# Softmax sums squared eight at a time, decay operands built four heads at a time, and a convolution tap on ScalarE, in a two-layer hybrid diffusion block on one core

## The chip, the core and the metric

The kernel runs on one core of one Trainium2 chip. The core has five engines that run their own instruction queues in order: TensorE (PE in the rows, its weight loads PEld), VectorE (DVE), ScalarE (ACT), GpSimd (POOL) and SyncE (SP, which here only issues DMAs). The metric is device microseconds of one execution. Everything told below about the kernel before comes from its times, its profile page, its trace and the order of its instructions.

## What is computed

Two layers over 1024 latent tokens and 256 context tokens of width 1024, all in float32. Cut to what matters here:

```python
for l in range(2):
    h = rms_norm(x) * (1 + sc1) + sh1
    q.., x_ssm, dt = split(h @ w_in[l])           # one wide projection
    y_na  = neighbourhood_attention(...)           # 4 heads
    y_df  = rms_norm(softmax(q1 k1) v - lam * softmax(q2 k2) v)   # 4 heads, "differential"
    u     = silu(depthwise_conv(x_ssm, 5 taps))    # the SSM's convolution
    y_ssm = ssd_chunked(u, dt)                     # 10 chunks of 128, 8 heads, both directions
    x = x + g1 * (concat(y_na, y_df, y_ssm) @ w_out[l])
    h = rms_norm(x) * (1 + sc2) + sh2
    gate, val = split(h @ w_up[l])
    x = x + g2 * ((silu(depthwise_conv(gate, 3 taps)) * val) @ w_down[l])
```

In the SSM, a decay matrix exp(cs_i - cs_j) of 128 by 128 is needed for each head, chunk and direction. In the differential attention the kernel never divides the scores by the first softmax sum s0: it lets the norm that follows cancel it, and for that adds 64 * eps * s0^2 to the mean square.

## The kernel before

The big projections are split into high and low parts, so that each product is three matmuls (lines 390 to 392 for the input, up and out projections, 1232 to 1234 for the down projection). For each weight block SyncE loads it, ScalarE rounds the high part (`wH`, line 240) and GpSimd subtracts to get the low part (`wL`, line 241).

The stages of a layer follow each other: the SSM's projections with their convolution (`xbc_conv`, lines 519 to 532, eight blocks of 128 channels); chunk states and the z projection; the projections of differential and neighbourhood attention, with the SSM's output (`ssd_out`, line 905) interleaved as a background stream (I call this the SSD stage); then the two attentions side by side (`df_stream`, line 678, and `natt`, line 1032); the output projection; the feed-forward part (`ffn`, line 1168), where for each of 22 blocks the gate is projected, convolved (line 1194 to 1198), passed through SiLU and multiplied into the value projection.

The order on each engine is not written by hand: a scheduler places instructions by priority and by its own estimate of times, and each engine then runs its own list in order, waiting at semaphores.

- Convolutions. ScalarE copies the projection from PSUM into a padded tile (`pad`, line 515; `fpad`, line 1184). VectorE computes the first tap with the bias (line 524, line 1194), then adds the other taps (line 527 four times, line 1197 twice) in place in `cacc` or `fa`. ScalarE applies SiLU.
- Decay. `decay(g)` (line 950) builds for two directions d and two halves e of a split number an operand `mf` of 128 by 4 heads by 128: a triangular mask times one column of `lah` for each head. Per tile that is four instructions of 128 columns, two on VectorE and two on GpSimd (line 958). A matmul (line 960) consumes each tile; there are three `mf` buffers. ScalarE then takes the exponential and VectorE multiplies it into `M` (line 965), which line 980 consumes. Over both layers there are 18 chunks, so 36 decays, 144 tiles and 576 instructions.
- Differential attention. A unit is one query tile of one head; there are 40 units in layer 0 and 32 in layer 1. For each, TensorE makes the scores of the two softmaxes (line 719, two PSUM buffers `s`), VectorE moves them out of PSUM with a running maximum (line 720), ScalarE takes exp and leaves the sums in `sums` (two columns), VectorE forms `rho` (lines 727 and 728) and the column 64 * eps * s0^2 in `dg` (line 733), GpSimd combines the two maps (line 736 scales, line 738 adds), TensorE transposes and multiplies with the values. After four query tiles, line 783 adds `dg` into the mean square.

Of the kernel before, what the change touches and what calls it, by code (L numbers as in the profile page):

```python
# [10 lines left out]
F32 = mybir.dt.float32  # L11
# [69 lines left out]
def hybrid_kernel(ctx, tc, xin, cc, w_ada, bada, gmf, w_in, w_dt, w_out, w_up, w_dn, vec, cst, rope, nab, out):  # L81
# [171 lines left out]

# [1 line left out]

# [72 lines left out]

# [1 line left out]
    def norm_temps(pool):  # L330
# [52 lines left out]

# [1 line left out]
    def proj_chunk(wh, wl, c0, n, evac, order=range(KT)):  # L385
# [45 lines left out]
    def dfproj(l, dfv, qchunks, lam, gq, gnq, sub, lam_init):  # L431
        NT = 10
        with phase(f"dp_{l}", "right") as p:
            rp = p.tile([128, 2, SEQ], F32, name="rp")
            SP.dma_start(out=rp, in_=rope)
            # lambda and gains
            lv = vc[:, l, V_LAM:V_LAM + 128].rearrange("p (a d) -> p a d", a=4)
# [45 lines left out]
    def mixer(l):  # L483
# [16 lines left out]

# [1 line left out]
        with phase(f"m1_{l}") as p:  # L502
            pads = []
            for i in range(2):
                pd = p.tile([128, 1288], F32, name=f"pad{i}")
                for a, b in ((0, 2), (1026, 1030), (1286, 1288)):
                    G.memset(pd[:, a:b], 0.0)
                pads.append(pd)

            def xbc_ev(b):  # L510
                pd = pads[b % 2]

                def ev(ps, c0, n):
                    o = 2 + c0 if c0 < SEQ else 1030
                    S.copy(out=pd[:, o:o + n], in_=ps)

                return ev

            def xbc_conv(b):
                pd = pads[b % 2]  # L520
                a = p.tile([128, 1284], F32, tag="cacc", name="cacc", bufs=2)
                cw = V_CW + 5 * b
                W = 1284 if full or b < 6 else SEQ
                V.tensor_scalar(out=a[:, 0:W], in0=pd[:, 0:W], scalar1=vcol(l, cw), scalar2=vcol(l, V_CB + b),
                                op0=ALU.mult, op1=ALU.add)
                for j in range(1, 5):
                    V.scalar_tensor_tensor(out=a[:, 0:W], in0=pd[:, j:j + W], scalar=vcol(l, cw + j), in1=a[:, 0:W],
                                           op0=ALU.mult, op1=ALU.add)
                act(out=a[:, 0:W], in_=a[:, 0:W], func=ACTF.Silu)
                SP.dma_start(out=ud[l][b, :, 0:SEQ], in_=a[:, 0:SEQ])  # L530
                if W > SEQ:
                    SP.dma_start(out=ud[l][b, :, SEQ:T], in_=a[:, 1028:1284])

            ws = w_pre if l == 0 else [load_w(w_in[l, B_XBC + b]) for b in range(2)]
            proj_many(ws, ALLC, [xbc_ev(b) for b in range(2)])
            for b in range(2):
                xbc_conv(b)
            if l == 0:
                side[0] = ada_stream(0, range(2, 5), asx.enter_context(phase("as", "right")))
            side_step(1)  # L540
            for b in range(2, 8):
                proj(w_in[l, B_XBC + b], ALLC if full or b < 6 else MAINC, xbc_ev(b))
                xbc_conv(b)
                side_step(1)

# [1 line left out]
        exp_tables()  # L547
        da = ExitStack()
        dfv = da.enter_context(phase(f"dfv{l}")).tile([128, NT, 256], F32, name="dfv")
        with phase(f"sw{l}") as sp:  # L550
# [58 lines left out]
          if True:  # L609
            p = sp  # L610
            ssd_states(l, p, dte, tot, full)

# [1 line left out]
            silu_tables()  # L614

            def zblk(b):
                def ev(ps, c0, n):
                    z = p.tile([128, 512], F32, tag="z", name="z", bufs=2)
                    act(out=z[:, :n], in_=ps, func=ACTF.Silu)
                    SP.dma_start(out=zd[l][b, :, c0:c0 + n], in_=z[:, :n])  # L620

                proj(w_in[l, B_Z + b], qchunks, ev)

            for b in range(4):
                zblk(b)
                side_step(2)
            side_finish()
            asx.close()
            exp_tables()
# [5 lines left out]

# [1 line left out]
        npx = ExitStack()  # L637
# [36 lines left out]
        nv_p = nvx.enter_context(phase(f"nv_{l}", "right"))  # L674
# [1 line left out]
        p = da.enter_context(phase(f"da_{l}"))  # L676

        def df_stream():
# [4 lines left out]
            po = {}  # L683
            dgs = {}

# [19 lines left out]
            def scores(b, qt, hh):  # L705
# [5 lines left out]
                es = []  # L711
                sums = p.tile([128, 2], F32, tag="sums", name="sums", bufs=4)
                for m in range(2):
# [3 lines left out]
                    for ci, (c, n) in enumerate(kch):  # L717
# [10 lines left out]
                V.scalar_tensor_tensor(out=rho, in0=rho, scalar=sums[:, 0:1], in1=lam,  # L728
                                       op0=ALU.mult, op1=ALU.mult)
                if hh == 0 and qt % 4 == 0:  # L730
                    dgs[b, qt // 4] = p.tile([128, 8], F32, tag="dg", name="dg", bufs=2)
                u = qt % 4 * 2 + hh
                V.scalar_tensor_tensor(out=dgs[b, qt // 4][:, u:u + 1], in0=sums[:, 0:1], scalar=64 * EPS, in1=sums[:, 0:1],
                                       op0=ALU.mult, op1=ALU.mult)
# [22 lines left out]
            def values(b, qt):  # L757
# [19 lines left out]
                sq, oh = tl("dsq"), tl("doh", F32R)  # L777
                act(out=sq, in_=pv, func=ACTF.Square)
                pm = pst("t", 2)[:, :n]
                PE.matmul(pm, C(C_BD64), sq, start=True, stop=False)  # L780
                for i in range(gn):
                    for hh in range(2):
                        PE.matmul(pm[64 * hh:64 * hh + 64, i * 128:(i + 1) * 128],
                                  dgs[b, qt // 4][:, 2 * i + hh:2 * i + hh + 1].to_broadcast([128, 64]), ident,
                                  start=False, stop=(i == gn - 1))
# [30 lines left out]

# [1 line left out]
        open_mm(ns=2, nt=1)  # L818
# [86 lines left out]
    def ssd_out(l, p, c, dts, lah, ecs):  # L905
# [44 lines left out]
        def decay(g):  # L950
            pd = pst("s", 2)
            i = 0
            for d, mk in ((0, C_PI), (1, C_SI)):
                for e in range(2):
                    mf = p.tile([128, 4, 128], F32R, tag="mf", name="mf", bufs=3)
                    for hh in range(4):
                        h = 8 * d + 4 * g + hh
                        (V if hh % 2 else G).tensor_scalar(out=mf[:, hh], in0=C(mk), scalar1=lah[:, e, c, h:h + 1], scalar2=1.0,
                                        op0=ALU.mult, op1=ALU.mult)
                    PE.matmul(pd, tri[:, d], mf.rearrange("p h i -> p (h i)"), start=(i == 0), stop=(i == 3))  # L960
# [205 lines left out]

# [1 line left out]
    def ffn(l, xt):  # L1168
# [3 lines left out]
        with phase(f"ffn{l}") as p:  # L1172
# [15 lines left out]
            def up(f, gate_done=False):  # L1188
                pad = pads[f % 2]
                if not gate_done:  # L1190
                    proj(w_up[l, 2 * f], chunks, gate_ev(f))
                a = p.tile([128, 1282], F32, tag="fa", name="fa", bufs=1)
                fw = V_FW + 3 * f
                V.tensor_scalar(out=a[:, :W], in0=pad[:, 0:W], scalar1=vcol(l, fw), scalar2=vcol(l, V_FB + f),  # L1194
                                op0=ALU.mult, op1=ALU.add)
                for j in range(1, 3):
# [89 lines left out]

# [1 line left out]
    with phase("n0") as p:  # L1288
# [165 lines left out]
```

## Time and profile before

| | |
|---|---|
| median of 3 runs | 3622.63 us (3618.60 to 3626.59) |
| profiled execution, first to last instruction (the only time that its profile gives) | 3627.4 us |
| TensorE busy | 3433.8 us, 95% |
| VectorE busy | 1950.4 us, 54% |
| GpSimd busy | 1446.3 us, 40% |
| ScalarE busy | 1242.3 us, 34% |
| mean granted TensorE clock | 0.975 |

Busy time is the union of an engine's instructions. "Granted clock" is the TensorE clock as a share of full speed (2.4 GHz; the lower level is 1.2 GHz). A wait row "PE x <- DVE y" sums the time in which TensorE stood idle just before x and what ended it was the end of y.

### The profile page before, as it was taken

To read this page: it belongs to the slowest core of one execution; us is meant where nothing else is said; L and a number is where in the kernel's file an instruction comes from. 1 tells how busy PE (TensorE), PEld (TensorE's weight loads), DVE (VectorE), ACT (ScalarE), POOL (GpSimd) and SP (SyncE) were. 2 spreads that over 40 slices of the span, in tenths; PEclk is the share of its full clock that TensorE was granted. 3 is DMA by queue.
4 is the path that set the end of the run, shared out by engine and by line. 5 is a ranking of instruction groups with operands and counts; after the bars stand their busy time and mean duration, and the time that the engine had idled before them with its cause. 6 is when DMAs were issued, how large, how long until landed. Compare 5 with 4: busy or idle time off the path is not lost. (4 is left out here: it accounts for less than half of the span.)

```text
span 3627.4 us, 49090 instructions
## 1 busy us (share of the span) xinstructions
PE 3433.8 (95%) x18762; PEld 2724.3 (75%) x18762; DVE 1950.4 (54%) x3816; ACT 1242.3 (34%) x2159; POOL 1446.3 (40%) x1092
## 2 busy tenths in 40 slices
PE   7998898899899999999999898998999999999999
PEld 3876676666678888888887676776666777887887
DVE  6735875787373343333335744885784633334333
ACT  4232433777341111111113333344675421221211
POOL 2136563666362222222222326673565532322332
PEclk8999999999999999999999999998999999999999
DMA  8255444753721111111112236447656211111111
GB/s 294 98 199 164 131 126 132 191 152 105 244 83 46 35 41 35 37 39 36 35 35 82 69 114 211 128 128 192 167 156 215 77 53 41 53 47 41 53 47 70
DMA packets 260202, 381.03 MB, mean 105 GB/s; under 512 B 20736, under 2 KB 161152, under 8 KB 259712
## 3 DMA queue, kind: packets, MB, share of 16 engines
q1 hardware_dynamic: 259968, 377.90, 33.8%
q8 instruction: 148, 2.42, 0.3%
q14 instruction: 86, 0.70, 0.1%
HBM read 294.72 MB, written 83.10 MB: 104 GB/s over the span
## 5 line engine op out<-in xcount | busy, mean ns | idle before, releaser
L390 PE MATMUL mm<-hH,wH 128*128 128x512 f32 (+1 forms) x2960 | 1117.6, 379 | 34.2 <-ACT wH L240 7.6
L391 PE MATMUL mm<-hL,wH 128*128 128x512 f32 (+1 forms) x2960 | 1113.2, 376 | 9.5 <-POOL hL L370 5.3
L392 PE MATMUL mm<-hH,wL 128*128 128x512 f32 (+1 forms) x2960 | 1111.4, 376 | 6.2 <-POOL wL L241 6.2
L241 POOL TENSOR_TENSOR wL<-wr,wH 128x1024 fp32r<-128x1024 f32 x220 | 533.2, 2429 | 1218.4 <-ACT wH L240 1195.3
L390 PEld LDWEIGHTS mm<-hH,wH 128*128 128x128 f32 x2960 | 564.7, 191 | 157.6 <-issue 15.1
L391 PEld LDWEIGHTS mm<-hL,wH 128*128 128x128 f32 x2960 | 564.4, 191 | 127.4 <-POOL hL L370 7.8
L392 PEld LDWEIGHTS mm<-hH,wL 128*128 128x128 f32 x2960 | 564.4, 191 | 114.8 <-POOL wL L241 7.7
L240 ACT CAST wH<-wr 128x1024 fp32r<-128x1024 f32 x220 | 228.3, 1048 | 808.1 <-PE mm L1233 471.9
L1237 DVE SCALAR_TENSOR_TENSOR xt<-mm,mods,xt 128x512 f32<-128x512 f32 (+1 forms) x440 | 300.9, 697 | 253.6 <-PE mm L1234 253.1
L1194 DVE TENSOR_SCALAR fa<-fpad,vc 128x1282 f32<-128x1282 f32 (+1 forms) x44 | 111.1, 2526 | 558.6 <-ACT fpad L1184 550.9
L1234 PE MATMUL mm<-gh,wL 128*128 128x512 f32 (+1 forms) x880 | 328.9, 374 | 0.0
L1232 PE MATMUL mm<-gh,wH 128*128 128x512 f32 (+1 forms) x880 | 325.0, 375 | 3.7 <-DVE xt L1237 3.6
L1233 PE MATMUL mm<-gl,wH 128*128 128x512 f32 (+1 forms) x880 | 326.9, 372 | 0.0
L720 DVE TENSOR_SCALAR_CACHE_REDUCE e<-s 128x512 f32<-128x512 f32 (+1 forms) x400 | 228.4, 588 | 88.2 <-PE s L719 85.6
L1208 POOL TENSOR_TENSOR gl<-fa,gh 128x512 fp32r<-128x512 f32 (+1 forms) x110 | 127.6, 1160 | 300.7 <-ACT gh L1207 300.7
L93 ACT ACTIVATE e<-e,nm 128x1280 f32<-128x1280 f32 (+1 forms) x144 | 182.9, 1271 | 53.6 <-DVE nm L723 48.5
L719 PE MATMUL s<-ks,qst 128*128 128x512 f32 (+1 forms) x400 | 161.5, 441 | 39.0 <-DVE e L720 23.4
L1232 PEld LDWEIGHTS mm<-gh,wH 128*128 128x128 f32 x880 | 164.5, 188 | 41.1 <-DVE xt L1237 8.7
L738 POOL TENSOR_TENSOR e<-e 128x1280 f32<-128x1280 f32 (+1 forms) x72 | 193.1, 2684 | 3.4
L1233 PEld LDWEIGHTS mm<-gl,wH 128*128 128x128 f32 x880 | 165.3, 188 | 32.7 <-issue 0.2
L1234 PEld LDWEIGHTS mm<-gh,wL 128*128 128x128 f32 x880 | 165.5, 188 | 32.1
L1206 DVE TENSOR_TENSOR fa<-fa,mm 128x512 f32<-128x512 f32 (+1 forms) x110 | 69.8, 635 | 209.3 <-PE mm L392 151.7
(269 smaller groups left out, 4930.1 us busy)
## 6 DMA issues: line engine op xcount, KB each, us to landing
wr<-in_w_up_dram SPq DMA_DIRECT2D x88, 512.0 KB
wa<-in_w_ada_dram SPq DMA_DIRECT2D x56, 512.0 KB
wr<-in_w_in_dram SPq DMA_DIRECT2D x48, 512.0 KB
wr<-in_w_dn_dram SPq DMA_DIRECT2D x44, 512.0 KB
wr<-in_w_ada_dram SPq DMA_DIRECT2D x40, 512.0 KB
wr<-in_w_out_dram SPq DMA_DIRECT2D x40, 512.0 KB
nbt<-in_nab_dram SPq DMA_DIRECT2D x64, 192.0 KB
ks<-qkd SPq DMA_DIRECT2D x16, 640.0 KB
```

The lines of the kernel that those rows point to most:

```text
L93: ins = S.activation(**kw)
L240: S.copy(out=wh, in_=wr)
L241: (eng or G).tensor_tensor(out=wl, in0=wr, in1=wh.bitcast(F32), op=ALU.subtract)
L390: PE.matmul(ps[:, :n], wh[:, ks], r, start=(i == 0), stop=False)
L391: PE.matmul(ps[:, :n], wh[:, ks], hsl(hL, k, c0, n), start=False, stop=False)
L392: PE.matmul(ps[:, :n], wl[:, ks], r, start=False, stop=(i == KT - 1))
L720: V.tensor_scalar(out=e[:, c:c + n], in0=s_, scalar1=1.0, scalar2=None, op0=ALU.mult, op1=ALU.max, accum_out=mx[:, ci:ci + 1])
L738: G.tensor_tensor(out=es[0][:, 0:nk], in0=es[0][:, 0:nk], in1=es[1][:, 0:nk], op=ALU.add)
L1232: PE.matmul(ps, wh[:, os_], gh[:, c0:c0 + n], start=(i == 0), stop=False)
L1233: PE.matmul(ps, wh[:, os_], gl[:, c0:c0 + n], start=False, stop=False)
L1234: PE.matmul(ps, wl[:, os_], gh[:, c0:c0 + n], start=False, stop=(i == len(hid) - 1))
L1237: V.scalar_tensor_tensor(out=xv, in0=ps, scalar=mods[l][:, 5, o, w:w + 1], in1=xv, op0=ALU.mult, op1=ALU.add)
```

## The change

Three edits. The first convolution tap with its bias becomes an affine activation on ScalarE, in both convolutions: 16 instructions of line 524 and 44 of line 1194 leave VectorE, 60 go to ScalarE. Each `mf` tile is one instruction of 128 by 512 with two broadcast operands, on one engine: of the four tiles of a decay GpSimd makes the first and the last, VectorE the two between. The sums of eight units (four query tiles, two heads) live in one tile, and one instruction squares all eight of them when the group's values are done: 72 instructions of one column become 10 of up to eight.

```diff
-                V.tensor_scalar(out=a[:, 0:W], in0=pd[:, 0:W], scalar1=vcol(l, cw), scalar2=vcol(l, V_CB + b),
-                                op0=ALU.mult, op1=ALU.add)
+                act(out=a[:, 0:W], in_=pd[:, 0:W], func=ACTF.Identity, scale=vcol(l, cw), bias=vcol(l, V_CB + b))
...
-                sums = p.tile([128, 2], F32, tag="sums", name="sums", bufs=4)
+                if hh == 0 and qt % 4 == 0:
+                    sgs[b, qt // 4] = p.tile([128, 8, 2], F32, tag="sums", name="sums", bufs=2)
+                u = qt % 4 * 2 + hh
+                sums = sgs[b, qt // 4][:, u]
...
-                if hh == 0 and qt % 4 == 0:
-                    dgs[b, qt // 4] = p.tile([128, 8], F32, tag="dg", name="dg", bufs=2)
-                u = qt % 4 * 2 + hh
-                V.scalar_tensor_tensor(out=dgs[b, qt // 4][:, u:u + 1], in0=sums[:, 0:1], scalar=64 * EPS, in1=sums[:, 0:1],
-                                       op0=ALU.mult, op1=ALU.mult)
...
                 act(out=sq, in_=pv, func=ACTF.Square)
+                s0 = sgs[b, qt // 4][:, 0:2 * gn, 0]
+                dg = p.tile([128, 8], F32, tag="dg", name="dg", bufs=2)
+                V.scalar_tensor_tensor(out=dg[:, 0:2 * gn], in0=s0, scalar=64 * EPS, in1=s0, op0=ALU.mult, op1=ALU.mult)
...
-                    for hh in range(4):
-                        h = 8 * d + 4 * g + hh
-                        (V if hh % 2 else G).tensor_scalar(out=mf[:, hh], in0=C(mk), scalar1=lah[:, e, c, h:h + 1], scalar2=1.0,
-                                        op0=ALU.mult, op1=ALU.mult)
+                    h = 8 * d + 4 * g
+                    (V if (d + e) % 2 else G).tensor_tensor(
+                        out=mf, in0=C(mk).unsqueeze(1).to_broadcast([128, 4, 128]),
+                        in1=lah[:, e, c, h:h + 4].unsqueeze(2).to_broadcast([128, 4, 128]), op=ALU.mult)
...
-                V.tensor_scalar(out=a[:, :W], in0=pad[:, 0:W], scalar1=vcol(l, fw), scalar2=vcol(l, V_FB + f),
-                                op0=ALU.mult, op1=ALU.add)
+                act(out=a[:, :W], in_=pad[:, 0:W], func=ACTF.Identity, scale=vcol(l, fw), bias=vcol(l, V_FB + f))
```

Since a scheduler sets the order, it moves other instructions too, mostly in the SSD stage and in the attentions. Three places carry the argument. Line numbers of the changed kernel differ by a few.

First, GpSimd in the first chunks of layer 0's SSD stage (`mf` the decay operands, `xd` and `yo` other operands of `ssd_out`, `qn` the rotary product of the attention's projection, `wL` a weight's low part). Before:

```order
L958 TENSOR_SCALAR mf<-cs,lah 128x128 x4
L926 TENSOR_TENSOR xd<-xt,dts 128x512 x2
L958 TENSOR_SCALAR mf<-cs,lah 128x128 x6
L465 TENSOR_TENSOR qn<-qn,rp 128x512
L947 TENSOR_TENSOR yo<-yo 128x512
L958 TENSOR_SCALAR mf<-cs,lah 128x128 x8
```

And with the change:

```order
L926 TENSOR_TENSOR xd<-xt,dts 128x512 x2
L465 TENSOR_TENSOR qn<-qn,rp 128x512
L947 TENSOR_TENSOR yo<-yo 128x512
L957 TENSOR_TENSOR mf<-cs,lah 128x512 x4
L241 TENSOR_TENSOR wL<-wr,wH 128x1024
```

GpSimd's list between two of its other jobs is now a run of two-input instructions of 512 columns and more, where small one-input instructions lay between them.

Second, VectorE in the attentions of layer 0 (`e<-s` moves scores out of PSUM, `nsb` belongs to the neighbourhood attention). Before:

```order
L720 TENSOR_SCALAR e,mx<-s 128x512
L733 SCALAR_TENSOR_TENSOR dg<-sums 128x1
L720 TENSOR_SCALAR e,mx<-s 128x256
L720 TENSOR_SCALAR e,mx<-s 128x512
L723 TENSOR_REDUCE nm<-mx 128x1
```

And with the change, around a stretch that corresponds to it and holds no such instruction:

```order
L730 SCALAR_TENSOR_TENSOR rho<-rho,sums,lam 128x1
L722 TENSOR_SCALAR e,mx<-s 128x256
L722 TENSOR_SCALAR e,mx<-s 128x512
L1097 TENSOR_SCALAR nsb,nmx<-ns 128x256
L725 TENSOR_REDUCE nm<-mx 128x1
```

One `dg` stood in each unit among the moves of the scores; with the change one stands in each group of eight.

Third, ScalarE at the first two blocks of layer 1's SSM convolution. Before:

```order
L240 CAST wH<-wr 128x1024
L515 COPY pad_17137<-mm 128x256
L240 CAST wH<-wr 128x1024
L515 COPY pad_17141<-mm 128x256
L93 ACT_TABLE_LOAD
L93 ACTIVATE cacc<-cacc 128x1284
L515 COPY pad_17137<-mm 128x512 x2
```

And with the change:

```order
L240 CAST wH<-wr 128x1024
L515 COPY pad_16829<-mm 128x256
L93 ACTIVATE cacc<-pad_16829,vc 128x1284
L240 CAST wH<-wr 128x1024
L515 COPY pad_16833<-mm 128x256
L93 ACTIVATE cacc<-pad_16833,vc 128x1284
L93 ACT_TABLE_LOAD
L93 ACTIVATE cacc<-cacc 128x1284
L515 COPY pad_16829<-mm 128x512 x2
```

The two taps stand directly behind the copies that they read; the copies of the third block stand behind the first SiLU as before.

## Rows read from the trace of the kernel before

**Rows 1.** The page: busy us by engine, share of the span, instructions.

```profile
PE 3433.8 (95%) x18762; PEld 2724.3 (75%) x18762; DVE 1950.4 (54%) x3816; ACT 1242.3 (34%) x2159; POOL 1446.3 (40%) x1092
```

**Rows 2.** Windows by stage: length, busy PE, PEld, DVE, ACT, POOL, clock, DMA, GB/s.

```profile
90.00:200.00 110.00, 110.00 (x580) 89.65 (x580) 74.66 (x47) 30.21 (x40) 19.29 (x8) 1.00 0.29 98
300.00:600.00 300.00, 270.21 (x1531) 208.00 (x1531) 229.57 (x470) 113.67 (x230) 183.27 (x233) 0.94 0.42 131
634.00:920.00 286.00, 256.95 (x2194) 189.30 (x2194) 222.69 (x860) 208.67 (x453) 181.39 (x125) 0.98 0.55 151
1075.00:1910.00 835.00, 835.00 (x4280) 704.77 (x4279) 308.96 (x360) 147.54 (x200) 207.01 (x120) 1.00 0.13 38
...
2250.00:2480.00 230.00, 213.80 (x1267) 167.29 (x1268) 182.99 (x368) 89.69 (x177) 147.53 (x188) 0.97 0.46 143
2500.00:2760.00 260.00, 238.25 (x2026) 175.16 (x2025) 205.30 (x783) 191.69 (x374) 167.51 (x99) 0.95 0.58 161
2905.00:3620.00 715.00, 714.86 (x3056) 572.89 (x3055) 261.88 (x281) 135.38 (x170) 204.28 (x106) 1.00 0.16 49
```

**Rows 3.** Waits of TensorE: total us, times, longest us.

```profile
PE s L719 <- DVE e L720: 23.4, 41, 2.1
...
PE s L1002 <- DVE yrs L1001: 8.6, 4, 3.9
...
PE mm L390 <- ACT pad L515: 7.2, 2, 6.2
...
PE o L980 <- DVE M L965: 6.3, 5, 2.3
...
PE s L960 <- DVE mf L958: 5.3, 3, 2.4
...
PE s L960 <- POOL mf L958: 2.0, 5, 0.6
```

**Rows 4.** Groups of instructions by form: busy us, mean ns, idle before.

```profile
L958 POOL TENSOR_SCALAR mf<-cs,lah 128x128 fp32r<-128x128 f32 x288 | 142.6, 512 | 48.3 <-PE s L960 47.5 <-POOL mf L958 0.4
...
L958 DVE TENSOR_SCALAR mf<-cs,lah 128x128 fp32r<-128x128 f32 x288 | 106.5, 429 | 19.7 <-PE s L960 19.4
...
L733 DVE SCALAR_TENSOR_TENSOR dg<-sums 128x1 f32<-128x1 f32 x72 | 67.2, 933 | 12.3 <-ACT e L93 12.2
...
L1194 DVE TENSOR_SCALAR fa<-fpad,vc 128x1282 f32<-128x1282 f32 x22 | 59.3, 2695 | 312.5 <-ACT fpad L1184 308.9 <-POOL gl L1208 3.7
...
L926 POOL TENSOR_TENSOR xd<-xt,dts 128x512 f32<-128x512 f32 x36 | 39.6, 1121 | 48.2 <-PE o L980 43.0 <-DMA xt<-xtd 5.2
...
L965 DVE TENSOR_TENSOR M<-M,cbl 128x512 f32<-128x512 f32 x36 | 31.3, 868 | 0.5
...
L93 ACT ACTIVATE cacc<-cacc 128x1284 f32<-128x1284 f32 x14 | 17.9, 1278 | 77.6 <-DVE cacc L527 67.3 <-issue 10.3
```

**Rows 5.** Timeline, attentions of layer 0: start, us, engine and instruction.

```profile
693.57 2.92 POOL L738 TENSOR_TENSOR e<-e 128x1280 f32<-128x1280 f32 x1
...
694.49 2.02 DVE L733 SCALAR_TENSOR_TENSOR dg<-sums 128x1 f32<-128x1 f32 x1 [1.52 <-ACT e L93]
...
697.17 0.39 PE L719 MATMUL s<-ks,qst 128*128 128x256 f32 x1 [1.98 <-DVE e L720]
```

**Rows 6.** Timeline, SSD stage of layer 0: VectorE beside a run of GpSimd.

```profile
561.52 1.29 POOL L660 TENSOR_TENSOR aqsq<-aqs,aoh 128x512 fp32r<-128x512 f32 x1
561.55 3.36 DVE L958 TENSOR_SCALAR mf<-cs,lah 128x128 fp32r<-128x128 f32 x3
...
562.78 2.04 POOL L926 TENSOR_TENSOR xd<-xt,dts 128x512 f32<-128x512 f32 x2
```

**Rows 7.** Timeline, first blocks of layer 1's SSM convolution.

```profile
2044.23 2.41 POOL L241 TENSOR_TENSOR wL<-wr,wH 128x1024 fp32r<-128x1024 f32 x1 [9.92 <-ACT wH L240]
2044.46 2.87 DVE L524 TENSOR_SCALAR cacc<-pad,vc 128x1284 f32<-128x1284 f32 x1 [9.74 <-ACT pad L515]
...
2050.86 0.94 DVE L524 TENSOR_SCALAR cacc<-pad,vc 128x1284 f32<-128x1284 f32 x1
```

More of the change, by code (lines that the diff above doesn't have):

```diff
@@ L683, in df_stream @@
             po = {}
-            dgs = {}
+            sgs = {}
             def load_k(b):
@@ L783, in values @@
                         PE.matmul(pm[64 * hh:64 * hh + 64, i * 128:(i + 1) * 128],
-                                  dgs[b, qt // 4][:, 2 * i + hh:2 * i + hh + 1].to_broadcast([128, 64]), ident,
+                                  dg[:, 2 * i + hh:2 * i + hh + 1].to_broadcast([128, 64]), ident,
                                   start=False, stop=(i == gn - 1))
```

## The prediction

> **What bounds the kernel now.** I read the page's busy times first: TensorE is busy 3433.8 of 3627.4 us [rows 1], and no part of the change adds or removes work there. So nothing can be gained beyond the 193.6 us in which TensorE stands idle, and what a lower clock costs. Next I cut the span into stages [rows 2]. In the feed-forward parts TensorE is busy 835.00 of 835 us and 714.86 of 715 us, and in layer 0's SSM convolution 110.00 of 110, all at full clock. The reader is to see that these stages offer nothing, although 52 of the 60 moved taps (44 and 8) stand there. What is left lies in four windows: the SSD stages (29.8 us idle in 300 at a clock of 0.94; 16.2 in 230 at 0.97) and the attentions (29.0 us in 286, 21.8 in 260). Then I read whom TensorE waits for [rows 3]. The largest single wait is that of the scores' matmul (line 719) for VectorE's move of earlier scores out of PSUM: 23.4 us in 41 pieces. Three waits belong to the decay and what VectorE runs beside it: line 1002 for `yrs` 8.6, line 980 for `M` 6.3, line 960 for `mf` 5.3 (VectorE) and 2.0 (GpSimd), together 22.2 us. One belongs to the convolution of layer 1: 7.2 us, of which 6.2 in one piece. That is the stock from which the change can draw directly: 52.8 us.
>
> **The convolution taps.** A tap that VectorE runs alone takes 0.94 us, and one that meets a GpSimd subtraction takes 2.87: it begins at 2044.46, while GpSimd's starts at 2044.23 and runs 2.41, and it ends just after that one [rows 7]. In the feed-forward part the mean is 2.70 us [rows 4], so that most taps meet one. On ScalarE I price a tap by the activation of the same 1284 columns, 1.28 us [rows 4]; it has two more per-partition operands, so this is a lower bound, and 2.87, what it replaces, is the upper.
>
> The Trainium skill speaks against this edit: the page "ScalarE: Activation LUTs", section "Rules for kernel authors", gives multiplication and addition to VectorE and not to ScalarE. By that rule and the row of a tap alone, the move would lose 0.34 us a tap, and the two taps ahead of layer 1's first SiLU (below) would make the term a loss of 0.7 us. By the row of a tap beside GpSimd a tap wins 1.59, and the mean of 2.70 us bears that out for most taps.
>
> None of that reaches TensorE in the 52 hidden taps. Their cover is the next projection's matmuls, which run on while the chain of taps and SiLU works; should the cover go, a tap costs at most its own 1.28 us, 44 times 1.28 or 56 us in all, and I see no reason for that, since the chain gets shorter. ScalarE waits in order, so what stands behind a tap are PSUM copies and weight casts; the tap reads what ScalarE wrote just before and waits for little else. In layer 1 the first SiLU holds up the copies of the third block, and these TensorE: the wait of 6.2 us. Ahead of that SiLU VectorE loses two taps, 2.87 and 0.94, together 3.81 us, while one tap of 1.28 comes in on ScalarE, and the next VectorE tap can still meet the second subtraction; I put 1 us on that. Term: 3.81 - 1.28 - 1 = 1.5 us gained, with bounds of 0 and 7.2.
>
> **The decay.** VectorE loses 288 instructions of 429 ns, 106.5 us, and gets 72 of 512 columns. The nearest row is `M` at line 965, two inputs from SBUF, one of them broadcast: 868 ns [rows 4], or 62 us. GpSimd loses 288 of 512 ns, 142.6 us, and gets 72, which I price by line 926, 512 columns with a broadcast operand: 1121 ns, or 81 us. So VectorE is relieved by 44 us and GpSimd by 62, over stages in which VectorE is busy 229.6 of 300 and 183.0 of 230 us [rows 2]. A decay's operands cost GpSimd 8 times 0.51 or 4.1 us before, in which all four tiles needed it, and 2.2 us now, in which two do. Against that stands what the order shows: GpSimd's list now has runs of long two-input instructions. In the trace VectorE gets no turn inside such a run: three small multiplications that begin at 561.55 take 3.36 us and end as GpSimd's run of 1.29 and 2.04 does [rows 6]. The Trainium skill says the same on the page "SBUF — State Buffer", section "Terms": the two engines share a port pair that is held for a whole instruction, and the loser blocks fully. By that rule alone the first rival below, 3638 us, would be the forecast; the rows agree as far as a run of two GpSimd instructions goes, and none shows a run of four tiles.
>
> So I do not credit the whole relief. Of the 22.2 us of waits I take a third, 7.4 us gained. The lower bound of the gain is a loss (the first rival); the upper is all 22.2. Each wait removed also spares part of the stretch at lower clock that goes with it: a mean clock of 0.94 over 300 us and of 0.97 over 230 is 18 and 7 us of full-speed time lost, against 46.0 us of idle time in the same windows. A removal of 7.4 in 46 takes 16% of 25 with it: 4 us, with bounds of 0 and 12 (22.2 in 46).
>
> **The squares.** 72 instructions of one column cost 933 ns each, 67.2 us [rows 4]. They are that long because they follow `rho` at once, and `rho` sets GpSimd's next job free or finds one running: at 694.49 one takes 2.02 us, and ends with GpSimd's 2.92 us addition that began at 693.57; the scores move only then, and TensorE has stood still for 1.98 us at 697.17 [rows 5]. Ten instead of 72 leave 58 us less on VectorE. Of the 23.4 us of waits I take 10 as gained; the rest has other causes (`rho` itself meets GpSimd in the same way and stays). Bounds: 0 and 23.4. What is added: the ten now stand right ahead of the matmuls that read them (line 783), so that TensorE may wait there. At 933 ns each and always waited for that is 9 us; the sums are ready by then and the scores' moves ahead of it are wanted anyway, so I put 2 us on it. The `sums` tiles have two buffers for groups of eight units, and GpSimd and ScalarE never wait for a whole group: nothing.
>
> **The sum.** -1.5 - 7.4 - 4 - 10 + 2 = -20.9 us, against the span of 3627.4: 3606.5. The median of the runs is 4.8 us below that span, so the median I expect is 3601.7, put at 3602 (-0.6%). A change of under 0.2%, 7 us, could not be told from none in this kernel: its three runs are spread over 8 us.
>
> **The rivals.**
> - *VectorE starves behind GpSimd (slower).* Place: `mf` and `M` on VectorE, while GpSimd runs its tiles, `xd`, `qn`, `yo` and `wL` in one run. Price: a run of four tiles is 4.5 us, and VectorE's tile, which the third matmul of the decay needs, comes after it. With 0.7 us more of waiting for each of 36 decays, 25 us, in place of the 11.4 gained there, the sum is -1.5 - 10 + 2 + 25 = +15: 3638. It is slower than before from 0.46 us a decay on (9.5 and 7 in 36). For it speaks the row of 3.36 us; against it that there are 72 instructions left on VectorE that can be caught, where there were 288, and that GpSimd is busy for 62 us less. Chance 0.13.
> - *The waits only change their name (no change).* TensorE is at 90% in the attentions, and ScalarE at 208.7 of 286 us; with VectorE out of the way the scores may wait for the exponential or a transposition instead, and a new order sets new waits. Then only the convolution and a little of the squares are left: -4, 3619. Chance 0.17.
> - *More goes than I credit.* If two thirds of the 52.8 us go and the clock stays up, 35 and 10 to 15 us: 3575. For it: the waits are single pieces of 2 us behind VectorE instructions of the kinds removed. Against: a matmul that need not wait for one thing mostly waits for the next. Chance 0.15.
> - *As summed*, -8 to -40 us: 3583 to 3615, chance 0.55.
>
> **How the numbers follow.** Faster by over 0.2%: the sum and the larger gain, 0.70. Within it: 0.17. Slower: 0.13. For 8 times in 10 the range leaves out the ends of the first and third rival: 3573 (the larger gain's middle) to 3629 (the upper edge of no change).
>
> **What would show it.** Right: line 719's wait for VectorE falls from 23.4 to about 13; the `dg` group is 10 instructions; `mf` costs VectorE some 62 and GpSimd some 81 us; the clock in 300 to 600 rises a little; the feed-forward windows stay full. Wrong: `mf` on VectorE at a mean above 1.3 us, line 960 or 980 waiting for more than 14 us together, or a new wait at line 783, or for ScalarE's `pad` or `fpad`. The most doubtful step is the third that I take at the decay.

## The result and the profile after

The changed kernel took 3669.57 us in the median, the kernel before 3624.61 us beside it: a ratio of 1.0115 [1.0096, 1.0133], so it is 1.15% slower, where a gain of 0.6% was forecast. In the text below a ratio always stands against runs of the kernel before on the same chip, and its interval of 95% in brackets.

The busy line of the page of the kernel after, whose span is 3666.5 us:

```profile
PE 3459.8 (94%) x18762; PEld 2742.5 (75%) x18762; DVE 1778.6 (49%) x3478; ACT 1324.3 (36%) x2219; POOL 1412.2 (39%) x876
```

Against [rows 1] VectorE is relieved by 172 us and GpSimd by 34, and ScalarE has 82 more. In kind that is what the edits say (of the 62 us that GpSimd was to be spared on `mf`, 47 are found). But TensorE, with the same 18762 matmuls, is busy 26.0 us longer, and idle 206.7 instead of 193.6 us. So of the 39.1 us between the two spans 13 are waiting and 26 are matmuls that ran slower: the mean granted clock fell from 0.975 to 0.964.

The windows of the kernel after (columns as in [rows 2]); but for the first, the bounds are moved so that the stages are the same ones:

```profile
300.00:600.00 300.00, 262.39 (x1481) 202.12 (x1479) 228.09 (x344) 111.62 (x226) 163.68 (x112) 0.92 0.40 126
634.00:938.00 304.00, 273.52 (x2214) 198.48 (x2213) 200.09 (x859) 215.68 (x464) 187.54 (x128) 0.92 0.50 142
1101.00:1936.00 835.00, 835.00 (x4280) 704.88 (x4279) 263.20 (x340) 176.77 (x219) 207.75 (x120) 1.00 0.13 38
2276.00:2520.00 244.00, 221.88 (x1293) 173.38 (x1294) 184.43 (x272) 89.62 (x178) 128.24 (x92) 0.94 0.45 138
2944.00:3659.00 715.00, 713.11 (x3049) 571.32 (x3048) 220.10 (x259) 159.82 (x189) 203.21 (x106) 1.00 0.16 49
```

The feed-forward windows are as full as they were [rows 2], but for 1.8 us in layer 1: the 44 taps there cost next to nothing. The first SSD stage, the attentions and the second SSD stage have a lower clock each (0.92, 0.92, 0.94, where it was 0.94, 0.98, 0.97).

The waits of TensorE in the kernel after:

```profile
PE t L464 <- DVE qn L461: 17.8, 7, 6.8
PE s L721 <- DVE e L722: 17.6, 30, 2.0
...
PE mm L390 <- ACT wH L240: 12.8, 7, 4.9
PE o L980 <- DVE M L965: 10.8, 10, 2.4
...
PE mm L390 <- DVE aqs L651: 7.9, 4, 3.8
PE mm L390 <- ACT pad L515: 6.2, 1, 6.2
PE mm L414 <- DVE aqs L651: 6.0, 4, 2.9
...
PE s L1002 <- DVE yrs L1001: 4.8, 4, 2.1
...
PE s L960 <- DVE mf L957: 4.4, 4, 2.6
PE s L960 <- POOL mf L957: 4.3, 3, 3.7
```

Of the waits in [rows 3] that of the scores fell from 23.4 to 17.6, the convolution's from 7.2 to 6.2, that for `yrs` from 8.6 to 4.8. That for `M` rose from 6.3 to 10.8 and that for `mf` from 7.3 to 8.7. The largest rises are in waits at which nothing was edited. In the kernel before these were:

```profile
PE t L464 <- DVE qn L461: 13.1, 3, 5.9
...
PE mm L390 <- ACT wH L240: 7.6, 3, 3.3
...
PE mm L390 <- DVE aqs L652: 3.2, 2, 2.9
...
PE mm L414 <- DVE aqs L652: 2.2, 2, 1.5
```

So the wait for the weights' rounding `wH` rose from 7.6 to 12.8 us, and in the SSD stage the waits for `qn` and `aqs`, which VectorE makes for the attentions' projections, rose from 13.1 to 17.8 and from 5.4 to 13.9.

The groups that answer to [rows 4], in the kernel after:

```profile
L957 POOL TENSOR_TENSOR mf<-cs,lah 128x512 fp32r<-128x512 f32 x72 | 95.7, 1346 | 61.9 <-PE s L960 58.3 <-DVE yrs L382 3.5
...
L957 DVE TENSOR_TENSOR mf<-cs,lah 128x512 fp32r<-128x512 f32 x72 | 73.4, 1024 | 28.3 <-PE s L960 28.2
...
L93 ACT ACTIVATE fa<-fpad,vc 128x1282 f32<-128x1282 f32 x22 | 32.2, 1463 | 4.8 <-POOL gl L1207 2.9
...
L778 DVE SCALAR_TENSOR_TENSOR dg<-sums 128x8 f32<-128x8 f32 x8 | 12.2, 1531 | 0.2 <-ACT e L93 0.2
```

The prices that were put on single instructions were a fifth too low for the decay (GpSimd 1346 ns instead of 1121, VectorE 1024 instead of 868), low for the new `dg` (1531 instead of 933) and right in kind for the taps (1463 ns, bound 1280). None of it is 40 us of TensorE's time. So the first question was which edit carries the loss.

### The profile page after: what moved, and what is told of

It is laid out like the page before. It is cut to its first block, busy times and chain, and to the rows that moved or that the text cites. A ratio compares the mean times of both kernels' runs of the same rounds, so it can differ in the third digit from the quotient of the medians.

```text
span 3666.5 us, 48430 instructions
## 1 busy us (share of the span) xinstructions
PE 3459.8 (94%) x18762; PEld 2742.5 (75%) x18762; DVE 1778.6 (49%) x3478; ACT 1324.3 (36%) x2219; POOL 1412.2 (39%) x876
## 5 line engine op out<-in xcount | busy, mean ns | idle before, releaser
L390 PE MATMUL mm<-hH,wH 128*128 128x512 f32 (+1 forms) x2960 | 1121.4, 380 | 39.1 <-ACT wH L240 12.8
L1196 DVE SCALAR_TENSOR_TENSOR fa<-fpad,vc,fa 128x1282 f32<-128x1282 f32 (+1 forms) x88 | 144.6, 1643 | 619.8 <-ACT fa L93 618.1
L721 PE MATMUL s<-ks,qst 128*128 128x512 f32 (+1 forms) x400 | 163.8, 451 | 31.4 <-DVE e L722 17.6
```

Source lines behind the costliest of these rows:

```text
L390: PE.matmul(ps[:, :n], wh[:, ks], r, start=(i == 0), stop=False)
```

## Experiments

### Each edit alone

`sq_only`:

```diff
-                V.scalar_tensor_tensor(out=dgs[b, qt // 4][:, u:u + 1], in0=sums[:, 0:1], scalar=64 * EPS, ...)
+                V.scalar_tensor_tensor(out=dg[:, 0:2 * gn], in0=s0, scalar=64 * EPS, in1=s0, op0=ALU.mult, op1=ALU.mult)
```

> The kernel before with the squares edit alone. Theory D (the decay operands made four heads at once carry the whole loss): 72 small VectorE instructions fewer, so 0 to 10 us faster than before. Theory P (each place has its own edit: the loss of 13 us in layer 0's attentions is the squares' own, since the dg instruction now stands between the values and the matmul that reads it): 8 to 15 us slower, all of it in layer 0's attentions. Theory R (no edit has a fixed price; what counts is the new order of the queues that any edit sets off): within 10 us either way, and the three edits alone don't add up to the 42 us.

`mf_only`:

```diff
-                    for hh in range(4):
-                        (V if hh % 2 else G).tensor_scalar(out=mf[:, hh], in0=C(mk), scalar1=lah[:, e, c, h:h + 1], ...)
+                    (V if (d + e) % 2 else G).tensor_tensor(out=mf, in0=C(mk)..., in1=lah[:, e, c, h:h + 4]..., op=ALU.mult)
```

> The kernel before with the decay operands made four heads at once alone. Theory D: 30 to 45 us slower, with the loss in both SSD stages and in layer 0's attentions. Theory P: 20 to 28 us slower, all of it in the two SSD stages, and layer 0's attentions as before. Theory R: anything within 15 us of no change.

`taps_only`:

```diff
-                V.tensor_scalar(out=a[:, 0:W], in0=pd[:, 0:W], scalar1=vcol(l, cw), scalar2=vcol(l, V_CB + b), ...)
+                act(out=a[:, 0:W], in_=pd[:, 0:W], func=ACTF.Identity, scale=vcol(l, cw), bias=vcol(l, V_CB + b))
```

> The kernel before with the first taps on ScalarE alone (the SSM convolution and the feed-forward). Theories D and P: within 5 us of no change, with the feed-forward windows full of TensorE work as before. Theory R: anything within 15 us of no change, through the SSD stage whose neighbours in the queues shift.

`squares_and_taps` has the first and the third of these.

> The changed kernel with the decay operands as they were before (one head at a time on both engines). Theory D: 0 to 12 us faster than before, that is 42 to 54 us faster than the changed kernel. Theory P: 8 to 15 us slower than before. Theory R: not the sum of the two edits measured alone.

Measured: squares 1.0028 [1.0018, 1.0038], 10 us slower; decay operands 1.0173 [1.0157, 1.0189], 62 us slower; taps 0.9999 [0.9989, 1.0010]; squares and taps 1.0021 [1.0011, 1.0031]. The decay operands lose most, as D says. But alone they lose more than all three edits together (42 us), and the squares, which only take work away, lose too. No theory fits all four: D expected 30 to 45 us of the decay operands and a gain of the squares, P expected no loss of the decay operands outside the SSD stages, and R at most 15 us. To see the places, the start of the n-th projection matmul (12480 of them, the same in all kernels) was compared between the trace of before and each other trace. What each stage takes more than before, in us:

```
                     SSD 0  attentions 0  out-proj. 0  SSD 1  attentions 1
after                  5.6          11.1          8.5   10.9           0.0
mf_only                6.3          13.5          9.6   11.0          12.1
sq_only               -1.2           4.1         -5.5   -0.1          17.2
```

In `mf_only` 35 of 54 us are lost in the attentions and the output projection, where no decay operand is computed. The price of a decay operand cannot act there directly. What an edit changes everywhere is the order: the scheduler places instructions by its own estimate of times, and each edit gave it other estimates.

### The order and the edits apart

From here on the order is taken from one kernel and the instructions from another. The scheduler makes the order of the one, and in the other each engine's instructions are chained to their neighbours in that order by dependencies that cost no wait. Only the edited instructions differ: taps and squares stand where the scheduler puts them.

```diff
+    order = _trace(lay, ORDER)[2]
+    nc, arrays, _ = _trace(lay, RUN, order)
...
+                        tc.add_manual_dep(ins, prev.name, info, reason="order")
```

`wide_old_order`:

```diff
+ORDER = (False, False, False)
+RUN = (True, False, False)
```

(the three flags are the decay operands, the squares and the taps)

> The decay operands made four heads at once alone, but every other instruction is issued on every engine in exactly the order of the kernel before; a wide operand stands where its engine's first narrow one of that tile stood. Theory O (the loss of 62 us of the wide operands comes from the new order that the scheduler makes of them): 0 to 20 us faster than before, since the operands cost 44 and 62 us less of VectorE and GpSimd. Theory I (it comes from the wide instructions themselves, which hold their engines for 0.7 to 2.8 us in one piece): 30 to 65 us slower than before.

`narrow_new_order`:

```diff
+ORDER = (True, False, False)
+RUN = (False, False, False)
```

> The reverse: the decay operands of the kernel before, one head at a time, but every other instruction in exactly the order that the scheduler made for the wide operands alone; the two narrow ones of an engine stand where the wide one stood, the other engine's two where the scheduler puts them. Theory O: 40 to 70 us slower than before, like the wide operands alone. Theory I: within 15 us of before.

`all_old_order`:

```diff
+ORDER = (False, False, False)
+RUN = (True, True, True)
```

> All three edits, with every unchanged instruction in the order of the kernel before. Theory O: the gain that was predicted, 5 to 30 us faster than before. Theory I: 25 to 50 us slower than before, like the changed kernel.

`none_after_order`:

```diff
+ORDER = (True, True, True)
+RUN = (False, False, False)
```

> None of the three edits, with every unchanged instruction in the order of the changed kernel. Theory O: 30 to 65 us slower than before. Theory I: within 15 us of before.

Measured: 1.0025 [1.0016, 1.0033], 1.0142 [1.0119, 1.0166], 0.9973 [0.9963, 0.9984] and 1.0133 [1.0117, 1.0149]. So the order of the changed kernel, with not one of its edits, costs 48 us, and the order that goes with the wide operands 51. The edits, in the old order, gain 10 us together. Theory O is borne out, with one miss: the wide operands in the old order do not gain but lose 9 us.

By the stages of the table above `none_after_order` takes 5.0, 14.5, 9.0, 10.1 and 7.0 us more than before: without any edit the losses stand where the changed kernel has them, and in layer 1's attentions, where that one loses nothing, too. The chains do what they should: in the traces of `none_after_order` and after, and of `all_old_order` and before, ScalarE, GpSimd and SyncE run the instructions that no edit touches in one sequence to the last, and so does TensorE but for two matmuls, VectorE but for five of 3396 instructions. No kernel was chained to its own order, which would show what the chains cost by themselves. But order and edits taken apart with them add up to 38 us for the three edits and 60 for the decay operands, and 42 and 62 were measured without them.

### The squares and the taps in the old order

`sq_old_order`:

```diff
+ORDER = (False, False, False)
+RUN = (False, True, False)
```

> The squares alone in the order of the kernel before. If the squares carry the 21 us of squares and taps, and the taps nothing: 17 to 24 us faster. If the taps have a part in it in this order: 8 to 15 us faster.

`sq_taps_old_order`:

```diff
+ORDER = (False, False, False)
+RUN = (False, True, True)
```

> The squares and the taps edited, the decay operands narrow, every unchanged instruction in the order of the kernel before. Theory O (an edit is worth what it is worth in the old order; the scheduler's new order costs the rest): the squares gain the 10 us of the prediction or somewhat more, the taps nothing, and the wide operands alone had lost 9 in the old order: 10 to 20 us faster than before, and 4 to 12 us faster than all three edits in the old order. Against it (the operands contribute to the gain of 8 us of all three): not faster than all three.

Measured: 0.9948 [0.9934, 0.9962], 19 us faster, and 0.9936 [0.9924, 0.9949], 3607.1 us, 23 us faster than before by the ratio, a little more than expected. The second is faster than both kernels, and its ratio is the lowest of all runs. In the order that the scheduler makes for the same two edits (`squares_and_taps`) they are 1.0021: 31 us between two orders of the same work. The intervals of the two kernels here overlap, so that nothing is shown of the taps. Busy line and wait of the scores in `sq_taps_old_order` (line 732 is the scores' matmul, 733 the move out of PSUM):

```profile
PE 3421.7 (95%) x18762; PEld 2717.6 (76%) x18762; DVE 1773.6 (49%) x3694; ACT 1325.2 (37%) x2219; POOL 1445.7 (40%) x1092
```

```profile
PE s L732 <- DVE e L733: 12.5, 27, 1.7
```

The wait went from 23.4 [rows 3] to 12.5 us. TensorE is idle 176.5 us (span 3598.2), 17 less than before, and its matmuls ran 12 us faster. But this execution took 3600.0 us, 7 below the median of its five.

### Where the new order costs

The order of before everywhere, none of the edits, and the new order in some stages alone. `order_ssd` (all that stands ahead of each layer's attentions), `order_att0` (layer 0's attentions and output projection) and `order_att1` (layer 1's attentions and output projection; by the trace no instruction behind them has another place than before):

```diff
+NEW = (True, True, True)
+MIX = (0, 2)
```

> None of the edits. Everything in the order of the kernel before, except what stands ahead of each layer's attentions (the SSD stages among it), which stands in the order of the changed kernel. If the order inside these stages costs by itself: 12 to 18 us slower than before, 4 to 5 in layer 0 and 10 in layer 1, and the attentions lose nothing. If the stages ahead set what the attentions lose: 30 to 50 us slower.

```diff
+NEW = (True, True, True)
+MIX = (1,)
```

> None of the edits. Everything in the order of the kernel before, except layer 0's attentions and output projection, which stand in the order of the changed kernel. If the order inside that stage costs by itself: 15 to 25 us slower than before, as this stage lost 23 us with the whole new order. If it lost them because work comes in late from the stage ahead: within 8 us of before.

```diff
+NEW = (True, True, True)
+MIX = (3,)
```

> None of the edits, the order of the kernel before, except layer 1's attentions and what follows them, in the order of the changed kernel. If the costs of the stages' orders add up to the 52 us of the whole new order, of which 24 and 17 were measured: 6 to 16 us slower than before. If the stages disturb each other: within 4 us of before.

Measured: 1.0041 [1.0028, 1.0053], 1.0064 [1.0051, 1.0077] and 1.0018 [1.0008, 1.0028], that is 15, 23 and 7 us. They add up to 45 of 48: each stage's order costs by itself. In `order_ssd`, without any edit, the waits for `qn` and `aqs` are up as in the changed kernel, by 11.3 us together; why VectorE comes late with them in that order was not traced:

```profile
PE t L467 <- DVE qn L464: 18.4, 6, 6.8
...
PE mm L393 <- DVE aqs L658: 6.0, 4, 3.4
...
PE mm L417 <- DVE aqs L658: 5.4, 4, 2.9
```

In `order_att0` the trace shows two kinds of cost. Windows of the kernel before, attentions and output projection of layer 0:

```profile
624.80:943.20 318.40, 283.62 (x2314) 209.16 (x2313) 235.08 (x901) 219.92 (x471) 192.89 (x131) 0.97 0.59 167
943.20:996.50 53.30, 49.77 (x203) 39.17 (x202) 20.38 (x21) 18.67 (x24) 21.68 (x9) 0.96 0.61 204
```

and the same two of `order_att0`:

```profile
624.60:955.50 330.90, 296.52 (x2318) 215.06 (x2317) 230.13 (x907) 222.68 (x473) 191.53 (x131) 0.93 0.52 153
955.50:1016.60 61.10, 53.61 (x204) 41.00 (x203) 22.68 (x22) 18.66 (x24) 23.79 (x10) 0.89 0.65 220
```

In the output projection TensorE is idle for 7.5 instead of 3.5 us and its clock is 0.89 instead of 0.96. The wait is one for weights. SyncE's and ScalarE's timeline of `order_att0` there (line 236 issues the load of a weight block, 243 rounds it):

```profile
943.50 4.99 SPq L1304 DMA_DIRECT2D xt<-in_xin_dram  x8
...
958.61 0.65 SPq L1301 DMA_DIRECT2D hL<-ydd  x1
...
960.67 0.33 SPq L236 DMA_DIRECT2D wr<-in_w_out_dram  x1
...
964.04 0.33 SPq L236 DMA_DIRECT2D wr<-in_w_out_dram  x1
...
966.56 1.05 ACT L243 CAST wH<-wr 128x1024 fp32r<-128x1024 f32 x1
...
970.30 1.05 ACT L243 CAST wH<-wr 128x1024 fp32r<-128x1024 f32 x1 [2.70 <-DMA wr<-in_w_out_dram]
```

and the waits of TensorE from 950 us on in `order_att0`, where before it had waited 1.8 us for `wH`:

```profile
PE mm L393 <- ACT wH L243: 6.0, 4, 2.8
```

The two weight loads stand behind the 16 loads of `hH` and `hL` that were issued from 948.78 to 958.61. In the order of before they stood ahead of those 16:

```profile
939.32 0.33 SPq L233 DMA_DIRECT2D wr<-in_w_out_dram  x1
...
942.45 0.33 SPq L233 DMA_DIRECT2D wr<-in_w_out_dram  x1
...
948.18 0.33 SPq L1272 DMA_DIRECT2D hH<-ydd  x1
```

In the attentions the reader is to see something else: the idle time is the same (34.8 and 34.4 us), and the whole 12.5 us are matmuls at a lower clock, 0.97 to 0.93. The new order does not bring more waiting there. That the same amount of waiting, at other moments, brings the clock down is what is left; it is argued here and not shown.

### Why the wide operands lose in the old order

`half_wide_old_order` has all three edits, but each tile is made in two halves on both engines at once:

```diff
+                        for eng, j in ((G, 0), (V, 2)):
+                            eng.tensor_tensor(out=mf[:, j:j + 2], in0=C(mk)..., in1=lah[:, e, c, h + j:h + j + 2]..., op=ALU.mult)
```

> All three edits in the old order, but each decay operand in two halves, two heads on GpSimd and two on VectorE at the same time. If the wide operands lose because one engine makes a whole tile, so that the tile comes later (1.5 us in one piece on GpSimd, against two pieces of 0.5 us side by side on both engines): the loss of 9 us goes, and the time is that of the squares and taps alone or up to 8 us better. If they lose because a multiplication of two inputs is slow on GpSimd and stops VectorE meanwhile, however long the piece: like all three edits in the old order, 3610 to 3622 us.

`wide_on_vector` and `wide_on_gpsimd` have the squares and the taps, and only one engine's tiles wide; the others are four narrow ones on both engines:

```diff
-                    if WIDE:
+                    if WIDE and (d + e) % 2 == 1:
```

> Squares, taps and, of the decay operands, only the tiles that the change gives to VectorE made wide; the tiles that it gives to GpSimd stay four narrow ones on both engines. Old order. Beside the squares and taps alone (21 us faster than before) and all three (8 us faster). If the wide multiplication on GpSimd, which makes VectorE wait, is what costs: 18 to 26 us faster than before. If the one on VectorE (1.13 us in one piece where two of 0.43 ran beside GpSimd's) is what costs: 6 to 12 us faster.

```diff
-                    if WIDE:
+                    if WIDE and (d + e) % 2 == 0:
```

> The reverse: only the tiles that the change gives to GpSimd made wide, VectorE's stay narrow on both engines. Squares and taps edited, old order. If the wide multiplication on GpSimd is what costs: 6 to 12 us faster than before. If VectorE's is: 18 to 26 us faster.

Measured: 0.9997 [0.9988, 1.0006], 0.9957 [0.9942, 0.9971] and 0.9987 [0.9978, 0.9996], where squares and taps with narrow operands have 0.9936. So halves side by side lose 22 us against narrow operands, wide ones on GpSimd 18, wide ones on VectorE 8 (its interval just overlaps), and wide ones on both 13 (`all_old_order`). The halves lose more than either of their expectations allowed (3627.67 us, where 3610 to 3622 was the slower one). The tile's lateness is not the cause, since the halves would have cured it: they take 814 ns on GpSimd and 723 on VectorE, side by side, where a wide tile takes 1319 or 1089. What fits the rows is that instructions with two inputs on GpSimd hold up VectorE beside them. TensorE's waits for `mf` and `M` together rank nearly in the same way (only the third and the fourth change places, whose intervals overlap): 11.8 us with narrow operands, 11.7 with wide ones on VectorE, 17.0 with wide ones on GpSimd, 19.1 with both and 19.8 with halves. The wait for `M`, in `sq_taps_old_order` and then in `all_old_order`:

```profile
PE o L1006 <- DVE M L991: 7.0, 6, 2.1
```

```profile
PE o L1006 <- DVE M L991: 10.6, 11, 4.0
```

The groups of `wide_on_vector`:

```profile
L978 DVE TENSOR_TENSOR mf<-cs,lah 128x512 fp32r<-128x512 f32 x72 | 61.0, 853 | 11.9 <-PE s L987 11.9
L985 DVE TENSOR_SCALAR mf<-cs,lah 128x128 fp32r<-128x128 f32 x144 | 45.7, 375 | 7.4 <-PE s L987 7.3
```

and of `wide_on_gpsimd`:

```profile
L985 DVE TENSOR_SCALAR mf<-cs,lah 128x128 fp32r<-128x128 f32 x144 | 87.1, 646 | 24.2 <-PE s L987 23.7
...
L978 POOL TENSOR_TENSOR mf<-cs,lah 128x512 fp32r<-128x512 f32 x72 | 80.8, 1142 | 24.7 <-PE s L987 23.3 <-DVE M L992 1.3
```

VectorE's narrow instruction has a mean of 375 ns where GpSimd's decay operands are narrow, and of 646 where they are wide. Part of this is the place, since the first run has them in the first and last tile of a decay and the second in the two between: with all four tiles narrow (`sq_taps_old_order`) the means are 384 and 510 there. So the wide tiles on GpSimd add 136 ns to each of 144 instructions, 20 us of VectorE's time. With both wide, VectorE's wide one rises from 853 to 1089 ns and GpSimd's from 1142 to 1319. A place in `all_old_order`, timeline, two engines and the matmuls that wait:

```profile
333.79 1.52 DVE L991 TENSOR_TENSOR M<-M,cbu 128x512 f32<-128x512 f32 x1
334.73 2.79 POOL L244 TENSOR_TENSOR wL<-wr,wH 128x1024 fp32r<-128x1024 f32 x1
335.24 2.83 DVE L978 TENSOR_TENSOR mf<-cs,lah 128x512 fp32r<-128x512 f32 x1
...
338.00 0.68 DVE L991 TENSOR_TENSOR M<-M,cbl 128x512 f32<-128x512 f32 x1
...
338.73 0.69 PE L1006 MATMUL o<-M,xd 128*64 128x128 f32 x3 [1.38 <-DVE M L991]
```

VectorE's `mf` begins inside GpSimd's subtraction, ends 0.55 us after it, and takes 2.83 us; `M` comes after it, and TensorE stands still. The Trainium skill says on the page "SBUF — State Buffer", section "SBUF: two separate sides", that an instruction of VectorE with two inputs can be shut out for the whole of a GpSimd instruction, and the rows agree.

## Why the prediction was wrong

**The step that failed is the sum itself.** Its terms were priced as if every other instruction kept its place. None stood for the new order, although the order of the changed kernel was known; the second rival said that "a new order sets new waits", and gave it the loss of gains, not a cost of its own (3619 us). Measured with none of the edits, that order costs 48 us. With it the sum would have been on the right side: 10 us gained in the old order and 48 lost make 38, and 42 were measured by the ratio. The clock term failed with it: 4 us were to come back at the decay, and over the whole kernel the matmuls took 26 us longer.

**The decay** was the second step, and its sign was wrong: 11.4 us of gain were credited, and in the old order 9 were lost with this edit alone, 13 beside the others. The relief of VectorE was counted as 44 us, with wide operands at 868 ns. In `wide_old_order` it is 26 on `mf`, and `M` takes 8 of them back (its means went from 835 and 868 to 991 and 934 ns). So the first rival had the mechanism, VectorE held up by GpSimd, and a price of 25 us in place of 11.4 gained; found were 9 to 13 us. Of the signs of being wrong one came, lines 960 and 980 waiting for more than 14 us together (19.5, where before it was 13.6), and the other did not, a mean above 1.3 us for `mf` on VectorE (1.02). That this rival had the kernel slower is for the most part luck: the order costs 48 us without a single wide operand, and the rival's price needs them.

**The squares** were right in mechanism and put too low: 10 us were credited and 19 measured in the old order. The wait was sized well (about 13 us left, 12.5 found). What the term left out is not settled. In the profiled execution of `sq_taps_old_order` other waits fell too, by some 6 of the 17 us, and the matmuls ran 12 us faster at a higher clock (0.978 instead of 0.975), which the prediction had counted for the decay alone. In that of `sq_old_order`, at 3620.43 us 12 above the median of its six, TensorE is busy for the same 3433.8 us as before, and all of the 8.9 us between the spans is waiting. The price of 2 us for the new `dg` was not needed: no wait of TensorE at the matmul that reads it is listed.

**The taps** were right where it mattered. The 44 in the feed-forward cost 1.8 us at most and the wait for `pad` fell by 1.0 us; the whole edit is within 4 us of no change, so that the term of 1.5 us cannot be told from nothing. By the Trainium skill's rule against such work on ScalarE (page "ScalarE: Activation LUTs", section "Rules for kernel authors") the kernel should have lost a little, 0.7 us as the prediction works it out; at 0.9999 [0.9989, 1.0010] neither that loss nor the gain could be seen.

**What stays open.** Why the new order costs is shown for layer 0's output projection, where weight loads went behind others in SyncE's queue. In the SSD stages it is shown which waits grow, and not why. In layer 0's attentions it is shown that the clock, not the idle time, makes the 12.5 us, but not which waits bring it down. Which of the scheduler's estimates leads it to the slower order was not tried. Nor is it shown that wide operands lose in every order: the old one was made for narrow ones.

## What to carry to other kernels

Where a scheduler sets the order, every edit is two changes, and the second can be several times the first. Run the edit in the old order, and the old instructions in the new one, before its price is believed; and keep a good order by pinning it. Few wide instructions with two inputs are no relief for VectorE where GpSimd works beside it: many narrow ones with one input were faster here by 13 us.

## What the runs showed of the hardware

The clock does not follow from the idle time alone: in layer 0's attentions TensorE is idle for 34.8 us before and 34.4 in `order_att0`, with a clock of 0.97 and 0.93. One place of the kernel after, in 4 us windows: a stretch with 1.39 us of work, in which TensorE begins to wait 2.83 us for the neighbourhood attention's `nk`, is followed by two at 0.67 and 0.50, in the second of which it was busy throughout:

```profile
652.00:656.00 4.00, 1.39 (x6) 0.56 (x4) 2.25 (x9) 3.17 (x6) 3.92 (x2) 1.00 0.98 238
656.00:660.00 4.00, 2.91 (x11) 2.22 (x12) 1.82 (x8) 0.00 (x0) 0.01 (x1) 0.67 1.03 253
660.00:664.00 4.00, 4.00 (x20) 2.72 (x19) 2.28 (x12) 3.62 (x7) 3.31 (x2) 0.50 1.09 333
```

In the kernel before, the stretch that answers to it has 1.77 us of work, with a wait of 2.33 us for `nk`, and the clock stays at full speed:

```profile
650.00:654.00 4.00, 1.77 (x17) 1.56 (x19) 2.19 (x9) 1.63 (x6) 3.92 (x2) 1.00 1.06 213
654.00:658.00 4.00, 3.24 (x35) 2.13 (x31) 2.08 (x11) 2.18 (x4) 0.65 (x2) 1.00 1.15 222
```

A clock of 0.50 is the lower of the two levels, 1.2 GHz. The two stalls are half a microsecond apart, and one of them was followed by matmuls at half the clock. Over the whole stage the same idle time of 34 us had a price 12.5 us apart in two orders of one work. Which waits bring the clock down, these rows do not tell.
